# Two-layer diffusion trunk on one core: how many steps of attention and of the time mixing's preparation are written beside each step of layer 0's projections

## The chip, the cores and the metric

One core of a Trainium2 chip runs the whole program. The metric is the device time of one execution in microseconds (us), as the median over runs. Beside the times there is a hardware profile of one execution; all engine times below come from it.

## The reference, cut to what matters

512 latent tokens and 256 context tokens of width 1024 go through two layers. Each layer has a mixer with two groups of heads and an MLP. The change lies in the mixer of layer 0. Its input projection gives both groups their inputs: the group of the time mixing (RWKV-7, a recurrence in both directions with a 64x64 state per head) and the group of the windowed attention (eight query heads over two key/value heads, a band of 128 tokens to either side, the context keys, and a sink logit).

```python
def even_mixer(u_ctx, u_lat, w_in, w_out, a_prm, sink, rope_ang, need_ctx):
    p_ctx = u_ctx @ w_in
    p_lat = u_lat @ w_in
    a_lat, a_ctx = rwkv7_mixer(p_ctx[..., :A_IN], p_lat[..., :A_IN], a_prm, need_ctx)
    ...
    b_lat = banded_window_attention(ql, kl, vl, kc, vc, sink_g)
    out_lat = jnp.concatenate([a_lat, b_lat], axis=-1) @ w_out
...
def rwkv7_scan(f, d, s0, reverse):
    def step(state, inp):
        r_t, w_t, k_t, v_t, kk_t, a_t = inp
        sa = jnp.einsum('bhvk,bhk->bhv', state, -kk_t)
        state = (state * w_t[:, :, None, :] + sa[..., None] * (kk_t * a_t)[:, :, None, :]
                 + v_t[..., None] * k_t[:, :, None, :])
        return state, jnp.einsum('bhvk,bhk->bhv', state, r_t)
```

The kernel doesn't step through the tokens. It cuts them into 12 chunks of 64, solves a triangular system within each chunk, and passes the state from chunk to chunk.

## The kernel before, in words

Everything is fp32; a weight is split into a high and a low part (`split`, lines 182 and 225: ScalarE writes the high part, VectorE the low one), and a product is three matmuls per 128 rows of the contraction. Tokens lie along the free dimension, features on the partitions.

**Generators and steps.** The program is written as Python generators. Each `yield` ends a step, and the code that drives them decides how many steps of one generator are written between two steps of another. Outside the opening, which is scheduled by hand, this order is a rank and not yet the order on an engine: a planner at compile time takes for each engine the instruction of the earliest rank among those whose inputs and buffers are there by its own estimate, so work of a later rank fills holes. On the chip each engine then follows its list in order, and a DMA queue does so too.

**The projections of layer 0.** `columns` (with `product`, line 430) makes 21 column blocks of 128 features; a block is two products, one for the 512 latent and one for the 256 context tokens, of 24 matmuls each. A step is 8 matmuls, so a block is six steps. Blocks 19, 20 and 15 come in the opening and block 16 in six steps of their own (`C0`); from there the counter `n` of the loop around the change starts at 24 and ends at 126. The blocks come in the order 17, 18, 0, 1, ... 14. `done` puts a block through ScalarE and, for blocks 0 to 14, two VectorE operations per product that mix in the neighbouring tokens (lines 1428 and 1429), and a DMA on ScalarE's queue stores it in the scratch tensor `scr`. The weights come through a `Stream`: `load` (line 238) issues 512 KB loads on SP's queue into two raw buffers, `ahead` splits them into three pairs of buffers.

**The attention of layer 0.** `attend` over `units_b`: four pairs of heads, six blocks of 128 queries each, so 24 items. An item has scores (lines 493 and 494), the two mask additions (656, 658), the maximum (499), the exponential (ScalarE), transposes of the probabilities (511), the product with the values (530) and a rescaling (531, 664), in a software pipeline of five steps per item. With eight steps of setting up, two at the start and four at the end it has 128 steps.

**The preparation of the time mixing.** `prep(p, ...)` for the four pairs p of heads. Up to the mark `FRONT` it has 12 steps: loads k and r (lines 849, 850), a norm (405, 415, and a power on GpSimd, 264), two low-rank products (865), two scans (877, 879), exponentials. From there to `READY` it has 18: the factors of the chunks (903 to 908 and 940 to 948; some on GpSimd) and the triangular matrices (917, 918), which go to DRAM and come back in another layout (925, 928; tile N). Then 15 steps hold an inversion of 31 pairs of dependent VectorE operations (954, 955), whose result is copied (958) and goes through DRAM again (959 to 967). Past the mark `MERGE` four steps merge 32x32 blocks into 64x64 ones (974, 982). `first` is the front of pair 0, the rest of pair 0 up to `MERGE`, and the front of pair 1: 57 steps. The buffers of the factors of pair 1 (`st1`) are opened on the side that the projections' inputs and weights have left.

**Behind the projections.** What is left of `first`, then the rest of pair 1 up to `READY`, then the merging of pair 0, with steps of `ada` (line 353 and 362: the modulation vectors of both layers, 80 loads of 512 KB on SP's queue) between them. Then comes for each pair the pass over the chunks (`chunks`, line 1023 first), with the next pairs' preparation beside it, and behind it the output projection and the MLP.

**The loop around the change** (in `trunk`, lines 1446 to 1460) drives the three: per step of the projections `RATE1` steps of attention; when the attention has ended and `n` is over 75, `RATE2` (1.5) turns per step go to `first`, in the order shown in the section on the change.

Of the kernel before, what the change touches and what calls it, by code (L numbers as in the profile page):

```python
# [25 lines left out]
NEG = -1.0e30  # L26
EM05 = math.exp(-0.5)

RATE1, RATE2, RATE3, RATE4, RATE5 = 2.0, 1.5, 1.8, 0.7, 0.5
QUIET = "quiet"  # L30
FRONT = "front"
READY = "ready"
# [142 lines left out]
def trunk(ctx: ExitStack, tc: tile.TileContext, xT, cT, vec_d, wada, we, wo_in, wout, wf1, wf2, lw2_d, la2_d, lg2_d,  # L175
# [5 lines left out]
    def act(o, i, f=AF.Copy, **k):  # L181
        return S.activation(o, i, f, **k)  # L182

    def pool(name, bufs=1, **k):
        return tc.tile_pool(name=name, bufs=bufs, reuse_waits="tile", **k)
# [26 lines left out]
    def one():  # L212
        if PS[0] is None:
            return wide()[:, 0:512]
        return PS[0].tile([128, 512], F32, name="x1")
# [219 lines left out]
    def columns(W, ms, uh, ul, done, parts=lambda m: ((0, L), (L, T))):  # L435

        for m in ms:
            w = W.take()
            for n, (a, b) in enumerate(parts(m)):
                ps = yield from product(w, uh, ul, a, b)  # L440
                if n == 0:
                    W.ahead(1)
                done(m, a, b, ps)
                yield
# [126 lines left out]
    def units(us, n):  # L571

        items = None
        g = us[0]
        while True:
            try:
                next(g)
                yield None
            except StopIteration as e:
                items = e.value  # L580
                break
        for u in range(len(us)):
            g, nxt = (us[u + 1] if u + 1 < len(us) else None), None
            for it in items:
                yield it
                for _ in range(n):
                    if g is not None:
                        try:
                            next(g)
                        except StopIteration as e:  # L590
                            g, nxt = None, e.value
            while g is not None:
                try:
                    next(g)
                    yield None
                except StopIteration as e:
                    g, nxt = None, e.value
            items = nxt
# [230 lines left out]
    def mix_lora(R):  # L829
        for j, a in enumerate((R["wl"], R["al"])):  # L830
            nc.sync.dma_start(a, scr[j])
        act(R["wl"], R["wl"], AF.Tanh)
# [421 lines left out]
    def drain(*gs, fill=lambda: None):  # L1254

        gs = list(gs)
        while gs:
            for g in list(gs):
                if next(g, gs) is gs:
                    gs.remove(g)  # L1260
            fill()
# [21 lines left out]
    def first():  # L1283
        yield from front(0)
        yield from until(preps[0], MERGE)
        yield from front(1)
    early = None
    with psum(2, 2), pool("pat", 2, space=PSUM) as pat, pool("wp", side="right") as wp, pool("ub", 1, side="right") as ub:
# [52 lines left out]
        with tc.manual_schedule(engines=ORDERED):  # L1341
# [27 lines left out]
            def some(ps, w, a, b, k0, k1):  # L1369
                for n, (x, y) in enumerate(three(lambda k: w[0][:, k, :], lambda k: w[1][:, k, :],  # L1370
                                                 lambda k: uh[k][:, a:b], lambda k: ul[k][:, a:b], k1, k0)):
                    PE.matmul(ps[:, 0:b - a], x, y, start=k0 + n == 0, stop=k1 == KT and n == 3 * (k1 - k0) - 1)
# [45 lines left out]
        with pool("po", 1, side="right") as pp:  # L1418
            bt = btx.enter_context(pool("bt", 1, side="right"))
            cur = {}  # L1420

            def done(m, a, b, ps):
                if a == 0:
                    cur[m] = pp.tile([128, T], F32, name="po", bufs=3)
                o = cur[m]
                if m < 15:
                    act(o[:, a:b], ps[:, 0:b - a], scale=om[:, m:m + 1])
                    stt(o[:, a + 1:b], ps[:, 0:b - a - 1], VV["mup"][:, m:m + 1], o[:, a + 1:b], op0=ALU.mult, op1=ALU.add)
                    stt(o[:, a:b - 1], ps[:, 1:b - a], VV["mun"][:, m:m + 1], o[:, a:b - 1], op0=ALU.mult, op1=ALU.add)
                else:  # L1430
                    act(o[:, a:b], ps[:, 0:b - a], scale=0.125 if m < 19 else 1.0)
                if b == T:
                    nc.scalar.dma_start(scr[m], o)
            for n, m in enumerate(ms[:3]):
                done(m, 0, L, first_ps[n])
            for n, m in enumerate(ms[:3]):
                ps = one()
                some(ps, ws[n], L, T, 0, KT)
                W.ahead(min(n + 1, 2))
                done(m, L, T, ps)  # L1440
            cg = columns(W, ms[3:], uh, ul, done)
            for _ in range(C0):
                next(cg)
            mk = lambda: pat.tile([128, 512], F32, name="ax")
            ab = attend(bt, units(units_b(bt), 1), mk, 5)
            n, due = 24, 0.0
            while next(cg, "end") != "end":
                n += 1
                due += RATE1 if ab else RATE2
                while due >= 1:  # L1450
                    due -= 1
                    if ab and next(ab, "end") == "end":
                        ab = None
                        btx.close()
                        rt, iv = (mixs[q].enter_context(pool(("rt", "iv")[q - 2])) for q in (2, 3))
                    if ab is None and n > 6 * 12 + 3:
                        if early is None:
                            mix_lora(R)
                            early = first()
                        next(early, None)  # L1460
            if ab:
                drain(ab)
                btx.close()
                rt, iv = (mixs[q].enter_context(pool(("rt", "iv")[q - 2])) for q in (2, 3))
            if early is None:
                mix_lora(R)
                early = first()
# [422 lines left out]
```

## Time and profile before

| | us |
|---|---|
| median of 3 runs | 2064.45 |
| lowest, highest run | 2062.24, 2076.95 |
| the profiled execution | 2066.39 |
| its span, first to last instruction | 2064.6 |
| TensorE busy in it | 1926.4 (93%) |
| VectorE busy | 1125.7 (55%) |
| ScalarE busy | 818.1 (40%) |

The span is the time from the first to the last instruction; 1.8 us of the execution lie around it. An engine's share is a mean over all stages: here the stages of layer 0's mixer have holes on TensorE, while the MLPs fill it, so the share alone doesn't tell what a change in one stage is worth. PEclk is the clock that TensorE was granted, as a part of 2.4 GHz; 0.5 is 1.2 GHz. PE is TensorE, DVE VectorE, ACT ScalarE, POOL GpSimd; PEld the loading of weights into the array; SPq SP's DMA queue.

### The profile page before, as it was taken

Reading aid. Unit: us, or ns where it says so; the run is one execution under the profiler, and the core shown is the slowest. Engines: PE = TensorE matmul, PEld = TensorE weight load, DVE = VectorE, ACT = ScalarE, POOL = GpSimd, SP = SyncE. Lnnn points to the kernel's source line nnn. Section 1 sums busy time; section 2 is a strip of 40 time slices with the busy share of each in tenths; the row PEclk is TensorE's granted clock in tenths of the full one; section 3 lists DMA queues with packets and bytes.
Section 4 is the critical chain, followed back from the end, with each engine's and each line's share of the span. In section 5 each row is a group of like instructions: output and inputs, shape, how many; then the busy total and the mean of one; then the engine's idle time right before and its main releaser. Section 6 shows DMA issues by size and latency. Waiting matters only on the chain.

```text
span 2064.6 us, 38578 instructions
## 1 busy us (share of the span) xinstructions
PE 1926.4 (93%) x16412; PEld 1630.6 (79%) x16412; DVE 1125.7 (55%) x1999; ACT 818.1 (40%) x1531; POOL 124.3 (6%) x149
## 2 busy tenths in 40 slices
PE   5999986798988899999999999899999899999997
PEld 3888774565667798888888889898888798888887
DVE  6576568556555468234433444865565676444445
ACT  3365533434335345312311232445686645222232
POOL 1000012001100000000000000001121000000000
PEclk9999988798898999999999999999999999999998
DMA  7421234676554223302221121332111425322321
GB/s 308 148 91 62 95 103 130 184 214 194 180 152 125 79 101 123 113 31 82 75 69 42 62 82 42 103 122 91 37 46 37 133 93 174 100 85 82 95 90 41
DMA packets 112012, 217.45 MB, mean 105 GB/s; under 512 B 38496, under 2 KB 63968, under 8 KB 111328
## 3 DMA queue, kind: packets, MB, share of 16 engines
q1 hardware_dynamic: 96544, 191.66, 28.9%
q10 hardware_dynamic: 15296, 23.33, 3.2%
q8 instruction: 128, 2.10, 0.4%
q14 instruction: 44, 0.36, 0.1%
HBM read 184.29 MB, written 28.05 MB: 103 GB/s over the span
## 4 chain that ended last, share of the span: by engine, by line
PE 63%; DVE 7%; ACT 3%; issue 2%; DMA 2%; POOL 1%; ACTq 0%; POOLq 0%; DVEq 0%; SPq 0%
PE x L1587 45%; PE x L430 5%; PE ax L530 2%; PE ax L511 2%; PE ad L353 1%; DMA w_raw<-in_wada_dram 1%; PE b L1015 1%; PE b L493 1%; PE b L494 1%; DVE pr L954 1%; PE b L1077 1%; DVE X L955 1%; DVE nacc L288 1%; ACT Z L182 0%; DVE MQ L1116 0%
## 5 line engine op out<-in xcount | busy, mean ns | idle before, releaser
L182 ACT ACTIVATE w_hi<-w_raw 128x1024 fp32r<-128x1024 f32 x183 | 192.1, 1057 | 476.6 <-PE x L1587 367.1
L225 DVE TENSOR_TENSOR w_lo<-w_raw,w_hi 128x1024 fp32r<-128x1024 f32 x181 | 222.1, 1230 | 196.7 <-ACT w_hi L182 196.1
L1587 PE MATMUL x<-fl,w_hi 128*128 128x256 f32 (+1 forms) x864 | 291.6, 339 | 3.9 <-DVE fl L1674 3.9
L1587 PE MATMUL x<-fh,w_lo 128*128 128x256 f32 (+1 forms) x864 | 289.9, 337 | 0.0
L1587 PE MATMUL x<-uh,w_hi 128*128 128x512 f32 (+1 forms) x864 | 286.9, 337 | 3.0 <-ACT uh L182 3.0
L1587 PE MATMUL x<-ul,w_hi 128*128 128x512 f32 (+1 forms) x864 | 287.4, 336 | 0.0
L1587 PE MATMUL x<-fh,w_hi 128*128 128x256 f32 (+1 forms) x864 | 287.3, 338 | 0.0
L1587 PE MATMUL x<-uh,w_lo 128*128 128x512 f32 (+1 forms) x864 | 287.1, 335 | 0.0
L1601 DVE TENSOR_TENSOR oa<-x,oa 128x512 f32<-128x512 f32 (+1 forms) x184 | 103.1, 563 | 207.7 <-PE x L1587 207.0
L430 PE MATMUL x<-uh,w_hi 128*128 128x256 f32 (+1 forms) x560 | 190.4, 340 | 0.9 <-ACT po L182 0.5
L430 PE MATMUL x<-uh,w_lo 128*128 128x256 f32 (+1 forms) x560 | 188.5, 337 | 0.0
L430 PE MATMUL x<-ul,w_hi 128*128 128x256 f32 (+1 forms) x560 | 188.5, 337 | 0.0
L1587 PEld LDWEIGHTS x<-fl,w_hi 128*128 128x128 f32 x864 | 165.1, 191 | 22.1 <-DVE fl L1674 4.5
L1587 PEld LDWEIGHTS x<-fh,w_lo 128*128 128x128 f32 x864 | 164.8, 191 | 17.8
L1587 PEld LDWEIGHTS x<-uh,w_hi 128*128 128x128 f32 x864 | 161.7, 189 | 21.2 <-ACT uh L182 3.9
L1587 PEld LDWEIGHTS x<-fh,w_hi 128*128 128x128 f32 x864 | 162.5, 190 | 19.9 <-ACT fh L182 2.5
L1587 PEld LDWEIGHTS x<-ul,w_hi 128*128 128x128 f32 x864 | 162.5, 189 | 17.7
L1587 PEld LDWEIGHTS x<-uh,w_lo 128*128 128x128 f32 x864 | 162.4, 189 | 17.6
L430 PEld LDWEIGHTS x<-uh,w_hi 128*128 128x128 f32 x560 | 107.2, 191 | 10.8 <-issue 1.1
L430 PEld LDWEIGHTS x<-uh,w_lo 128*128 128x128 f32 x560 | 107.3, 192 | 9.2 <-issue 1.0
L430 PEld LDWEIGHTS x<-ul,w_hi 128*128 128x128 f32 x560 | 107.2, 191 | 8.5 <-issue 0.5
L1673 DVE TENSOR_TENSOR rl<-rl 128x512 f32<-128x512 f32 (+1 forms) x108 | 59.3, 551 | 73.8 <-ACT fh L182 73.6
(304 smaller groups left out, 3383.7 us busy)
## 6 DMA issues: line engine op xcount, KB each, us to landing
w_raw<-in_wf_dram SPq DMA_DIRECT2D x128, 512.0 KB
w_raw<-in_wada_dram SPq DMA_DIRECT2D x96, 512.0 KB
w_raw<-in_we_dram SPq DMA_DIRECT2D x21, 512.0 KB
w_raw<-in_wo_in_dram SPq DMA_DIRECT2D x18, 512.0 KB
w_raw<-in_wout_dram SPq DMA_DIRECT2D x16, 512.0 KB
hsc<-h ACTq DMA_DIRECT2D x8, 1024.0 KB
scr<-po ACTq DMA_DIRECT2D x21, 384.0 KB
h<-hsc SPq DMA_DIRECT2D x7, 1024.0 KB
```

Of the source, the lines that this page charges most:

```text
L182: return S.activation(o, i, f, **k)
L225: eng.tensor_tensor(o_lo, x, o_hi.bitcast(F32), op=ALU.subtract)
L288: V.tensor_reduce(acc, sq.rearrange("p k t -> p t k"), axis=AX.X, op=ALU.add)
L353: PE.matmul(ps[o:o + 32, 0:256], si[:, 2 * kp + k, :], w[:, k, j * 256:(j + 1) * 256], start=kp == 0, stop=kp == 3)
L430: PE.matmul(ps[:, 0:b - a], x, y, start=j == 0, stop=j == len(pairs) - 1)
L493: PE.matmul(ps[:, off:off + n], qs, kh, start=True, stop=False)
L494: PE.matmul(ps[:, off:off + n], qs, kl, start=False, stop=True)
L511: PE.transpose(pt[:, (kb - k0) * 128:(kb - k0 + 1) * 128], P[:, kb * 128:(kb + 1) * 128], ident)
L530: PE.matmul(po[h * 64:h * 64 + 64, 0:128], v(h, k), pts[h][:, k], start=k == 0, stop=k == n - 1)
L1587: PE.matmul(o, a, b, start=n == 0, stop=n == len(pairs) - 1)
L1601: tt(oa[:, m, tok], ps, oa[:, m, tok], op=ALU.add)
L1673: tt(r, r, r, op=ALU.mult)
```

## The change

Two places: the number of attention steps per step of the projections goes from 2 to 3, and each turn of the preparation is two steps and not one. `RATE1` is used at this place alone.

```diff
-RATE1, RATE2, RATE3, RATE4, RATE5 = 2.0, 1.5, 1.8, 0.7, 0.5
+RATE1, RATE2, RATE3, RATE4, RATE5 = 3.0, 1.5, 1.8, 0.7, 0.5
...
             while next(cg, "end") != "end":
                 n += 1
                 due += RATE1 if ab else RATE2
                 while due >= 1:
                     due -= 1
                     if ab and next(ab, "end") == "end":
                         ab = None
                         btx.close()
                         rt, iv = (mixs[q].enter_context(pool(("rt", "iv")[q - 2])) for q in (2, 3))
                     if ab is None and n > 6 * 12 + 3:
                         if early is None:
                             mix_lora(R)
                             early = first()
-                        next(early, None)
+                        for _ in range(2):
+                            next(early, None)
```

## Rows read from the trace of the kernel before

**Rows 1.** Windows: length, busy us of PE, PEld, DVE, ACT, POOL, clock, DMA share, GB/s

```profile
97.00:253.00 156.00, 155.12 (x1147) 128.36 (x1146) 101.55 (x253) 91.38 (x220) 8.08 (x26) 1.00 0.24 82
254.00:295.00 41.00, 33.14 (x236) 26.28 (x237) 29.64 (x34) 17.29 (x25) 9.51 (x4) 0.83 0.35 119
334.00:376.00 42.00, 18.88 (x371) 12.26 (x370) 24.89 (x51) 8.91 (x18) 9.48 (x6) 0.60 0.69 195
376.00:462.00 86.00, 77.34 (x1386) 53.28 (x1388) 50.28 (x115) 33.95 (x65) 6.58 (x9) 0.96 0.64 196
```

**Rows 2.** Timeline of PE, 253 to 376 us: start, us, what, idle before

```profile
256.60 2.40 PE L405 MATMUL x<-con,t 128*128 128x2 f32 x12 [3.00 <-ACT t L182]
...
290.14 1.14 PE L917 MATMUL b<-ar,bk 64*64 64x64 f32 x32 [5.13 <-DVE XI L918]
...
301.19 0.40 PE L430 MATMUL x<-uh,w_hi 128*128 128x512 f32 x1
...
309.53 0.40 PE L430 MATMUL x<-uh,w_hi 128*128 128x512 f32 x1
...
333.91 0.28 PE L430 MATMUL x<-uh,w_lo 128*128 128x256 f32 x1
...
367.55 2.76 PE L974 MATMUL b<-xw,XI 32*32 32x32 f32 x92 [1.85 <-DMA xw<-tscr]
...
375.92 1.54 PE L1023 MATMUL b<-con,bk 128*128 128x128 f32 x6
```

**Rows 3.** Timeline of DVE, 255 to 385 us

```profile
292.13 0.68 DVE L918 TENSOR_TENSOR XI<-b,con 128x512 f32<-128x512 f32 x1
...
309.04 0.18 DVE L954 TENSOR_TENSOR pr<-X,N 96x31 f32<-96x31 f32 x1
...
357.86 1.03 DVE L958 COPY N<-X 96x1024 f32<-96x1024 f32 x1
374.91 0.19 DVE L954 TENSOR_TENSOR pr<-X,N 96x31 f32<-96x31 f32 x1 [16.02 <-DMA N<-nscr]
```

**Rows 4.** Groups of DVE, 309 to 360 us: busy us, mean ns, idle before

```profile
L955 DVE TENSOR_TENSOR X<-X,pr 96x31 f32<-96x31 f32 (+15 forms) x31 | 12.9, 417 | 0.5
L954 DVE TENSOR_TENSOR pr<-X,N 96x31 f32<-96x31 f32 (+15 forms) x31 | 10.4, 336 | 0.4
...
L1429 DVE SCALAR_TENSOR_TENSOR po<-x,vec,po 128x511 f32<-128x511 f32 (+1 forms) x6 | 3.6, 607 | 0.0
```

**Rows 5.** Groups of PE, ACT and DVE in the attention's stretch, 97 to 253 us

```profile
L430 PE MATMUL x<-uh,w_hi 128*128 128x256 f32 (+1 forms) x145 | 50.3, 347 | 0.0
...
L182 ACT ACTIVATE P<-b,nmx 128x513 f32<-128x513 f32 (+2 forms) x48 | 31.3, 654 | 22.6 <-DVE nmx L499 15.9 <-DVE b L660 4.8 <-DVE sm L554 0.9
...
L225 DVE TENSOR_TENSOR w_lo<-w_raw,w_hi 128x1024 fp32r<-128x1024 f32 x9 | 11.0, 1222 | 2.2 <-ACT w_hi L182 2.0
```

**Rows 6.** Windows of layer 1's attention, columns as in rows 1

```profile
1508.00:1560.00 52.00, 51.21 (x418) 42.23 (x417) 36.91 (x62) 43.07 (x89) 14.63 (x14) 1.00 0.09 27
...
1612.00:1664.00 52.00, 45.49 (x380) 40.60 (x378) 24.38 (x45) 27.72 (x59) 2.17 (x6) 1.00 0.33 104
```

**Rows 7.** Timeline of SP's DMA queue, 200 to 440 us: start, time of the issues

```profile
281.83 0.33 SPq L849 DMA_DIRECT2D k<-scr  x1
282.91 0.33 SPq L238 DMA_DIRECT2D w_raw<-in_we_dram  x1
```

**Rows 8.** Waits of SP's queue, 200 to 420 us: total, times, longest

```profile
SPq L849 <- POOL t L940: 26.4, 2, 23.4
```

**Rows 9.** Timeline of POOL, 60 to 440 us

```profile
247.89 0.95 POOL L930 MEMSET X<- 96x1024 f32 x1
...
336.88 2.02 POOL L940 TENSOR_TENSOR kds<-ic,k 128x768 f32<-128x768 f32 x1 [14.76 <-ACT ic L182]
...
342.87 4.07 POOL L940 TENSOR_TENSOR t<-ic,k 128x768 f32<-128x768 f32 x1 [3.49 <-issue]
348.15 1.82 POOL L947 TENSOR_TENSOR kds<-kds,t 128x768 f32<-128x768 f32 x1 [1.21 <-DVE bk L942]
```

## The prediction, made before the changed kernel was run

> **What bounds the kernel now.** I first read the windows over layer 0's mixer [rows 1]. While the attention runs beside the projections (97 to 253 us) TensorE is busy 155.12 of 156 us at full clock: nothing is to be had there but a different mixture of the same work. Between 334 and 376 us it is busy 18.88 of 42 us, at a mean clock of 0.60. That is the hole the change can reach. The timeline of TensorE [rows 2] gives its edges: the last matmul of the projections starts at 333.91, and the pass over the chunks of pair 0 starts at 375.92. VectorE's timeline [rows 3] says what holds the hole open: the matrices of pair 0 are done at 292.81, their return through DRAM lets the inversion start at 309.04, it ends with the copy at 357.86 to 358.89, its result goes through DRAM again, and only at 367.55 do the merges start on TensorE. So the end of layer 0's mixer hangs on one chain: front of pair 0, matrices, DRAM, inversion, DRAM, merges, chunks. TensorE's other work (the projections) runs out 42 us before this chain is through. Smaller losses stand at the chain's start: 3.00 us before the norm of pair 0 and 5.13 us at the third group of matrices [rows 2], in a stretch with a clock of 0.83 [rows 1].
>
> **The change, part by part.** No instruction is added or removed. What moves is the rank of the attention's and of the preparation's steps, and with it the place of their DMAs on SP's queue.
>
> *Counting.* A step of the projections on TensorE is a sixth of a block: (309.53 - 301.19)/6 = 1.39 us [rows 2], alone and at full clock. The stretch of 97 to 253 us holds 3 x 145 = 435 of its matmuls [rows 5] (the other two groups of line 430 count 145 each too), that is 435/8 = 54.4 steps or 75.6 us. The remaining 156 - 75.6 = 80.4 us are the attention's. Since a block ends at 253 us with n = 90, n was about 36 at 97 us.
>
> *Three attention steps.* Before, 128 steps at two per step end at n = 24 + 64 + 1 = 89; after, at n = 24 + 43 = 67. TensorE's work up to any n stays the same, only sorted differently, so at n = 76 the clock on the wall shows 97 + 80.4 + (76 - 36) x 1.39 = 233.4 us. The same sum to n = 90 gives 252.5, where the trace has 253.
>
> *Two steps of preparation.* The gate `n > 75` never bound before, since the attention ended at 89. Now it does: `first` begins at n = 76. Its norm matmuls, at 256.60 before [rows 2], come at about 234. At 1.5 turns of two steps the 57 steps are all written by n = 95, where they took until n = 126.
>
> *The chain, moved.* From the norm to the last matrix it took 292.81 - 256.60 = 36.2 us. Most of this is waiting from engine to engine, so I leave its length: 234 + 36 = 270. DRAM took 309.04 - 292.81 = 16.2 us: N is there at 286. The inversion was stretched to 48.8 us because VectorE had 51 us of work in that time [rows 4] (the smaller groups of that view left out there): 23.3 for the inversion itself (12.9 + 10.4), 6.5 for the projections' mixing (3.6 of them in line 1429), 5.3 for the front of pair 1, 14.2 for pair 1's factors, and small ones. Now the factors of pair 1 can't be there yet: their buffers need the projections' room. When do the projections end? From 233.4 on TensorE has 50 x 1.39 = 69.5 us of them, about 9 for pair 0's front and matrices, 6 for pair 1's front, and 5 of stall as before: 323 us. At 286 some four blocks are left, which cost VectorE four times (four mixings of 0.61 [rows 4] and one split of 1.22 [rows 5]), 14.6 us. Inversion 20.8 (see the port, below), front of pair 1 5.3, blocks 14.6: 41 us, so the inversion ends at 327 and its copy at 328. From the copy's end to the main merges it took 367.55 - 358.89 = 8.7 us, from there to the chunks 375.92 - 367.55 = 8.4. The chunks start at 345, where they started at 375.9: 30 us earlier.
>
> *What is late next, and what is given back.* Between 323 and 337 TensorE has only pair 1's matrices and the modulation's matmuls, so a hole of some 14 us stays. Pair 1's factors (14.2 us of VectorE) start at 323 and end near 342, before the first VectorE work of the chunks. Its inversion, from 375 on before [rows 3], would run from about 362 inside pair 0's chunks (345 to 431) as it did before. The modulation's matmuls that filled the old hole must go elsewhere: at most their 9 us at the low clock, at least nothing, since pair 0's chunks leave 8.7 of 86 us idle [rows 1]; I take 3.
>
> *A denser attention.* Where TensorE finds the attention not ready it waits, because its list is fixed. Before it lost 0.9 us in the stretch. After, the same 80.4 us of attention lie beside 31 steps instead of 54, in about 123 us. ScalarE was busy 91 of 156 us [rows 1]; if all 91 were the attention's, that is 74% of 123. Lower bound nothing. Upper bound: where layer 1's attention runs short of projections TensorE idles 6.5 of 52 us [rows 6], which for 123 us is 15. The nearer row is the one in which ScalarE is busy 83% and TensorE still 51.21 of 52: 1.5%, so I take 2 us.
>
> *SP's queue.* The load of pair 1's k (281.83) waited 23.4 us for GpSimd to release pair 0's [rows 8], and a weight load stood right behind it [rows 7]. After the change more weight loads stand behind such waits: three blocks' more. The cover is two raw and three split buffers, some 25 us or more of projections at 8.3 us per block. I cost it at nothing; without the cover the price is a wait of up to 23 us.
>
> *The port of VectorE and GpSimd.* The inversion's 31 updates (line 955) took 417 ns in the mean, its 31 products of the same sizes (954) 336 ns [rows 4]: 2.5 us more in all, while GpSimd worked 2.02 + 4.07 + 1.82 = 7.9 us on pair 1's factors [rows 9]. I read the difference as the cost of that neighbour. After the change these three operations come behind the inversion, hence 23.3 - 2.5 = 20.8. The Trainium skill (SBUF — State Buffer, Who interferes with whom) goes further: it says that a VectorE operation with two SBUF inputs and a GpSimd one that reads SBUF exclude each other for a whole instruction. By that rule up to the whole 7.9 us would be freed, and the forecast would be 5 us lower; the rows show only 2.5 of it.
>
> **Sum.** 30 - 3 - 2 = 25 us. From the profiled execution, 2066.4 - 25 = **2041 us**; the median of the runs is 2 us below that execution, which I leave in the range. Behind layer 0's mixer the page has TensorE busy nine tenths in nearly every slice, so a shift there arrives at the end.
>
> **The rivals.**
>
> *Half of it.* The inversion stays as slow as it was (48.8 us from 286, since its operations alternate with whatever else is ready), and N comes up to 6 us later because more weight loads share the DMA queue. The copy ends at 341, the chunks start at 358: 18 us, less 5 given back: 13, 2053 us. For it: VectorE was without a hole there. Against it: 14 us of that work can't start yet.
>
> *Nothing moves.* The planner fills holes beyond the written order: pair 0's X was cleared at 247.89 [rows 9], before the attention's end. If it had already pulled everything as early as it can go, the rank changes nothing: 2064 us. Against it: TensorE was full until 253, so there rank decided.
>
> *Slower: the attention starves TensorE.* In the stretch from 97 to 220 us the chain scores, maximum, exponential, transposes of an item doesn't keep up with three steps. If TensorE idles there as in the poor window [rows 6] it costs 15 us, and if its clock falls to the 0.83 of the stretch with such holes [rows 1], 0.17 x 123 = 21 more. Against a gain of 27 without the attention's term this ends at 2066 + 36 - 27 = 2075 us. It decides against the change from 27 us on, 1.1 us for each of 24 items. Against it: less than 1 us of waits at two steps.
>
> *More.* The inversion runs almost undiluted and the 5.13 us stall and the low clock around 260 us vanish: 36 us, 2030 us.
>
> **How the numbers follow.** Forecast 0.43, half 0.25, nothing 0.13, slower 0.08, more 0.11. One per cent is 20.6 us, about what a measurement of this kernel can tell from none: the forecast passes it four times in five (0.35), "more" always, "half" one time in five (0.05): faster 0.51. The starving attention passes it on the other side less than half the time, and I add a little for an order that falls badly: 0.05. The rest, 0.44, is within it. The range leaves out the far part of "more" and the slower half of the starving: 2026 to 2066.
>
> **What would show it.** Right: attention's last item near 220 to 225, line 405 near 234, the inversion's first operation near 286, the chunks' first transposes near 345, the projections ending near 323, and from there on all stages shifted by the same amount. Wrong: waits of TensorE on ScalarE or VectorE between 97 and 225 (starving), line 405 still near 256 (nothing moves), an inversion that ends past 335 (half), or a pass over pair 0's chunks that takes more than the 86 us it took (given back).

## The result, and the profile after

The kernel after takes 2056.1 us (median of 14 runs, 2047.9 to 2069.0), the kernel before 2066.8 beside it (14 runs, 2057.0 to 2078.5): a ratio of 0.995, interval 0.993 to 0.9969, some 10 us faster. The forecast was 2041. The direction was right, the 25 us were more than twice the gain. The profiled execution took 2055.19 us with a span of 2053.4.

Windows of after, columns as in [rows 1]:

```profile
97.00:226.00 129.00, 128.68 (x975) 103.24 (x974) 86.76 (x234) 81.45 (x209) 9.34 (x26) 1.00 0.23 74
...
243.00:253.00 10.00, 9.53 (x23) 5.00 (x24) 5.20 (x6) 2.50 (x3) 0.00 (x0) 0.50 0.25 92
...
288.00:304.00 16.00, 16.00 (x42) 9.94 (x41) 12.43 (x26) 9.24 (x12) 0.00 (x0) 0.50 0.00 0
304.00:346.00 42.00, 42.00 (x248) 36.78 (x246) 28.26 (x64) 9.69 (x15) 2.96 (x3) 1.00 0.37 107
346.00:365.00 19.00, 13.05 (x339) 9.12 (x338) 14.28 (x21) 6.39 (x15) 4.69 (x3) 0.75 0.73 213
365.00:449.00 84.00, 74.22 (x1372) 53.50 (x1370) 51.64 (x118) 34.56 (x65) 6.68 (x9) 0.96 0.63 197
```

The denser attention ends at 226 us almost without a hole (128.68 of 129). The hole of 42 us in [rows 1] has become one of 19, and the pass over pair 0's chunks is no longer than before. But two stretches stand among the projections in which TensorE is full and its clock is 0.50, that is 1.2 GHz: 9.53 + 16.00 us of work there would take half as long at full clock, 12.8 us less. The timeline of TensorE says what stands in front of each:

```profile
238.80 1.47 PE L405 MATMUL x<-con,t 128*128 128x2 f32 x12
...
243.47 1.54 PE L415 MATMUL b<-con,t 128*128 128x128 f32 x6 [1.98 <-DVE t L412]
244.94 2.93 PE L865 MATMUL b<-wl,lw 64*128 64x512 f32 x4
...
287.47 1.51 PE L415 MATMUL b<-con,t 128*128 128x128 f32 x6 [2.36 <-DVE pr L954]
288.91 4.10 PE L865 MATMUL b<-wl,lw 64*128 64x512 f32 x8
...
303.54 0.63 PE L430 MATMUL x<-uh,w_lo 128*128 128x512 f32 x1
...
304.33 0.40 PE L430 MATMUL x<-ul,w_hi 128*128 128x512 f32 x1
...
345.78 0.28 PE L430 MATMUL x<-uh,w_lo 128*128 128x256 f32 x1
...
348.81 0.69 PE L917 MATMUL b<-ar,bk 64*64 64x64 f32 x8 [2.40 <-DVE po L1429]
352.08 1.12 PE L917 MATMUL b<-ar,bk 64*64 64x64 f32 x28 [2.59 <-DVE bk L908]
...
357.05 1.99 PE L974 MATMUL b<-xw,XI 32*32 32x32 f32 x96
...
364.70 1.54 PE L1023 MATMUL b<-con,bk 128*128 128x128 f32 x6
```

Behind each norm (line 405) the transposes (415) wait 1.98 and 2.36 us, and the clock is down to half from there on; after the second wait a matmul of 512 columns takes 0.63 us until 303.54 and 0.40 from 304.33. The projections end at 346, later than the 334 of [rows 2]. The main merges start 10.5 us and the chunks 11.2 us earlier than in [rows 2]. VectorE's timeline:

```profile
268.60 0.68 DVE L918 TENSOR_TENSOR XI<-b,con 128x512 f32<-128x512 f32 x1
...
287.24 0.18 DVE L954 TENSOR_TENSOR pr<-X,N 96x31 f32<-96x31 f32 x1
...
329.90 1.13 DVE L958 COPY N<-X 96x1024 f32<-96x1024 f32 x1
...
381.44 0.18 DVE L954 TENSOR_TENSOR pr<-X,N 96x31 f32<-96x31 f32 x1
```

Against [rows 3] the matrices are 23 us earlier, the inversion starts 22 and its copy 28 us earlier. So pair 0's chain came as far ahead as forecast, and lost 17 us of it between the copy and the chunks: the merges wait behind pair 1's matrices (line 917) in TensorE's list, and these wait for the end of the projections.

### The profile page after: what moved, and what is told of

Read it like the earlier page. It is cut to its first block, busy times and chain, and to the rows that moved or that the text cites. A ratio compares the mean times of both kernels' runs of the same rounds, so it can differ in the third digit from the quotient of the medians.

```text
span 2053.4 us, 38620 instructions
## 1 busy us (share of the span) xinstructions
PE 1932.7 (94%) x16412; PEld 1633.5 (80%) x16412; DVE 1124.7 (55%) x1999; ACT 817.0 (40%) x1531; POOL 122.2 (6%) x149
## 4 chain that ended last, share of the span: by engine, by line
PE 63%; DVE 7%; ACT 3%; issue 3%; DMA 2%; POOL 1%; POOLq 0%; ACTq 0%; DVEq 0%; SPq 0%
PE x L1588 45%; PE x L430 5%; PE ax L530 2%; PE ax L511 2%; PE b L1015 1%; PE b L493 1%; PE ad L353 1%; PE b L1077 1%; PE b L494 1%; DMA w_raw<-in_wada_dram 1%; DVE X L955 1%; DVE nacc L288 1%; ACT Z L182 1%; DVE pr L954 1%; POOL r L264 0%
```

## The experiments

The table has what the timelines of TensorE show: the end of the projections, the first transposes of pair 0's first and second batch of chunks, and the first merges of pairs 1 and 3 (us). A ratio is to the runs of before that were taken beside the kernel's own. The marks come from the one profiled execution, which can lie up to 10 us from the median (att2_prep2_vkr 2074.2 against 2063.8, after_late_ada 2065.1 against 2071.8): marks of two kernels that lie few us apart tell nothing.

| kernel | median (runs) | ratio, interval | proj. end | batch 1 | batch 2 | merges 1 | merges 3 |
|---|---|---|---|---|---|---|---|
| before | 2066.8 (14) | | 334 | 375.9 | 390.5 | 462.6 | 637.2 |
| after | 2056.1 (14) | 0.995, 0.993 to 0.9969 | 346 | 364.7 | 375.8 | 448.3 | 622.3 |
| att3_prep1 | 2077.8 (12) | 1.0047, 1.0031 to 1.0064 | 348 | 366.9 | 410.7 | 479.1 | 650.7 |
| att2_prep2 | 2065.6 (12) | 0.9996, 0.9979 to 1.0012 | 342 | 363.4 | 397.4 | 468.1 | 640.9 |
| room16 | 2059.7 (12) | 0.9955, 0.9934 to 0.9975 | 331 | 347.8 | 387.8 | 454.9 | 626.1 |
| merge_first | 2054.2 (8) | 0.9935, 0.9912 to 0.9958 | 348 | 365.6 | 375.6 | 445.2 | 625.3 |
| room16_late_ada | 2059.4 (12) | 0.9971, 0.9952 to 0.999 | 332 | 348.5 | 365.0 | 440.6 | 629.7 |
| after_late_ada | 2071.8 (10) | 1.0021, 1.0004 to 1.0038 | 348 | 363.5 | 374.9 | 440.6 | 635.2 |
| before_late_ada | 2080.9 (4) | 1.0071, 1.0055 to 1.0088 | 335 | 374.7 | 386.7 | 455.6 | 652.1 |
| room16_v | 2056.5 (4) | 0.9945, 0.9923 to 0.9967 | 329 | 345.7 | 379.8 | 454.4 | 625.2 |
| room16_spread | 2066.5 (12) | 0.9991, 0.9969 to 1.0012 | 330 | 347.0 | 363.5 | 435.6 | 634.0 |
| after_spread | 2080.4 (7) | 1.0054, 1.003 to 1.0077 | 347 | 363.2 | 374.3 | 444.3 | 647.7 |
| room16_merge_spread | 2058.9 (12) | 0.996, 0.9942 to 0.9979 | 328 | 344.2 | 355.0 | 424.0 | 622.3 |
| **room16_vkr** | **2043.1 (6)** | 0.9861, 0.9833 to 0.9889 | 330 | 348.0 | 360.8 | 434.1 | 607.0 |
| after_vkr | 2053.4 (7) | 0.9934, 0.9908 to 0.9959 | 347 | 366.5 | 376.4 | 448.8 | 620.1 |
| before_vkr | 2072.5 (12) | 1.0015, 0.9998 to 1.0033 | 335 | 377.0 | 391.5 | 465.2 | 634.9 |
| room_merge_vkr | 2045.2 (6) | 0.9881, 0.9857 to 0.9906 | 334 | 353.9 | 364.7 | 433.9 | 607.4 |
| att3_prep1_vkr | 2055.2 (5) | 0.993, 0.9907 to 0.9954 | 341 | 361.5 | 375.0 | 449.9 | 626.7 |
| att2_prep2_vkr | 2063.8 (10) | 0.9979, 0.9961 to 0.9997 | 340 | 367.0 | 378.8 | 465.0 | 638.0 |

**The halves of the change, alone.**

```diff
-RATE1, ... = 2.0, ...                          # att3_prep1, from before
+RATE1, ... = 3.0, ...
-RATE1, ... = 3.0, ...                          # att2_prep2, from after
+RATE1, ... = 2.0, ...
```

> The attention's half of the change alone: three attention steps, one step of preparation per turn. Theory A (the change's gain comes from the attention making room, and the second step per turn only costs TensorE waits and clock between 239 and 304 us): line 405 stays near 239, the waits before line 415 are no longer than 2 us in all, the projections end between 333 and 342 (346 with both halves), the chunks start between 352 and 362, time 2045 to 2054. Rival B (the second step per turn is what brings the chain forward): N and the inversion come 8 us or more later than with both halves (N at 295 or later), the chunks start at 365 or later, time 2056 to 2063.

> The preparation's half alone: two attention steps, two steps of preparation per turn. Theory A: line 405 at 256 as before, since the attention still ends at n = 89; the projections end at or after 334 (before: 334) because of added waits before line 415; the chunks start between 368 and 380, time 2058 to 2070, no better than 0.5% under the kernel before. Rival B: most of the gain is here, chunks at 366 or earlier, time 2052 to 2058.

Neither half gains, and one loses, though both start the chunks 9 and 12 us earlier than before. In both the second batch comes 44 and 34 us behind the first, against 15 in before. Why had to stay open here; the last two runs answer it for att3_prep1 and in part for att2_prep2. Att3_prep1 is slower than both its theory and its rival; att2_prep2 has the time of its theory, with chunks that start as early as its rival had them. The waits in front of line 415 are there in both: 1.98 and 1.73 us in att3_prep1, 1.72 and 1.35 in att2_prep2. So it isn't the second step of the preparation alone that brings them.

**Room between the norm and its transposes.** In the list of after only six and seven projection matmuls stand between lines 405 and 415 (in before eight, at the low clock, and eleven, without a wait over 0.9 us), and in that time GpSimd's power (2.27 us) and two short VectorE operations have to come. Room16 writes 16 empty steps there.

```diff
         pow_mhalf(r12[:, :2 * nt], n12[:, :2 * nt], 2 * nt)
-        yield
+        for _ in range(1 + room):              # room=16 for pairs 0 and 1, else 0
+            yield
```

> Both halves, and 16 empty steps in the preparation of pairs 0 and 1 between the norm's matmuls (line 405) and the transposes that wait for GpSimd's power (line 415 in the changed kernel). They put some 35 matmuls of the projections behind the norm where 6 and 7 stood. Theory A (TensorE's end of the projections moved from 334 to 346 us because of the waits for the power and the low clock that follows each): both waits before the transposes gone (4.4 us), TensorE at full clock from 282 to 304 in place of 0.5, the projections end between 332 and 339, the chunks start between 348 and 358, time 2042 to 2051. Rival C (the waits are short and the low clock has another cause, such as the small matmuls of the low-rank products): the waits go but the clock stays low there, the projections end at 341 or later, time 2053 to 2058. Rival D (the chain of the time mixing is the bound, not TensorE): the empty steps delay the chain by 5 us, the chunks start at 368 or later, time 2058 to 2063.

The first half of the matter is settled by windows of room16 that answer to those of after:

```profile
239.00:270.00 31.00, 28.47 (x244) 22.96 (x243) 21.40 (x29) 14.28 (x22) 6.57 (x4) 1.00 0.25 85
270.00:310.00 40.00, 38.13 (x209) 30.51 (x208) 34.17 (x63) 18.60 (x24) 3.68 (x2) 1.00 0.42 129
...
348.00:455.00 107.00, 89.99 (x1454) 60.80 (x1456) 53.78 (x122) 35.83 (x68) 7.25 (x10) 0.82 0.69 211
```

The waits in front of the transposes are gone, the clock is 1.00 throughout beside the same low-rank matmuls (rival C falls), and the projections end at 331 instead of 346: 15 us, against 4.3 of waits and 12.8 of low clock in after. The chunks start at 347.8, 28 us before [rows 2]. Yet nothing of this arrives: the pass over pair 0 takes 107 us instead of the 86 of [rows 1].

**Merges first.**

```diff
-        for t in until(preps[1], READY):
-            next(ag, None)
         for t in preps[0]:
             next(ag, None)
+        for t in until(preps[1], READY):
+            next(ag, None)
```

> Both halves, and the merges of pair 0 written before pair 1's matrices behind the projections instead of after them. Theory A (from 346 on the chunks wait because the merges, whose data is there by 339, stand behind pair 1's matrices in TensorE's list): the merges start between 346 and 349 (357 with the change), the chunks between 352 and 358 (364.7), time 2046 to 2052. Rival E (pair 1's matrices have to be done anyway, and the time moves into the pass over the chunks): the chunks start early but the merges of pair 1 (448 with the change) don't come earlier by over 3 us, time 2054 to 2059.

The merges start at 350.9 instead of 357.1, the chunks at 365.6 as in after, and its time can't be told from that of after, as rival E had it: with projections that end at 348, the order behind them makes no difference that shows.

**Where room16 loses it: the modulation.** Timeline of TensorE in room16, between the two batches:

```profile
357.26 0.73 PE L353 MATMUL ad<-w_raw,si 128*32 128x256 f32 x8 [2.37 <-DMA w_raw<-in_wada_dram]
359.39 1.08 PE L353 MATMUL ad<-w_raw,si 128*32 128x256 f32 x8 [1.41 <-DMA w_raw<-in_wada_dram]
...
373.57 2.03 PE L353 MATMUL ad<-w_raw,si 128*32 128x256 f32 x16 [0.33 <-DVE mod L364]
375.96 0.89 PE L1041 MATMUL b<-con,vr 128*128 128x128 f32 x3 [0.37 <-POOL vr L1039]
...
387.82 1.54 PE L1024 MATMUL b<-con,bk 128*128 128x128 f32 x6
```

and of SP's queue in room16:

```profile
355.51 14.31 SPq L341 DMA_DIRECT2D w_raw<-in_wada_dram  x8
369.87 0.43 SPq L1001 DMA_DIRECT2D v<-scr  x1
370.35 0.42 SPq L850 DMA_DIRECT2D k<-scr  x1
```

For 18 us TensorE has only the modulation (`ada`, line 353), and a load at a time to wait for. The load of v that pair 0's chunks need stands behind eight modulation loads on the queue. In after it went at 344.65, in before at 332.78. Three kernels write the modulation's steps elsewhere, a fourth moves the load of v.

```diff
         for t in until(preps[1], READY):       # late_ada, spread
-            next(ag, None)
+            pass
         for t in preps[0]:
-            next(ag, None)
+            pass
...
-                due[1] += RATE4                # RATE4 = 0.7
+                due[1] += RATE4                # late_ada: RATE4 = 0.95
+                due[1] += 1.3 if p == 0 else RATE4   # spread: RATE4 = 0.7
```

```diff
-        nc.sync.dma_start(v, scr[3 + 3 * p + 2])              # room16_v, in chunks
+        (nc.sync if p else nc.scalar).dma_start(v, scr[3 + 3 * p + 2])
```

> Room16 with one more edit: none of the modulation's steps is written beside the preparation that stands between the projections and the chunks; the rate beside the chunks goes from 0.7 to 0.95 so that all are still written before the end. Theory (in room16 a bunch of 40 modulation matmuls, each four of them waiting for a 512 KB load, stands in TensorE's list between the first and the second batch of pair 0's chunks, and eight such loads stand on SP's queue ahead of the load of v): the projections end near 331 and the chunks start near 347 as in room16, the second batch's first transposes follow within 14 us instead of 39, the merges of pair 1 start near 436 instead of 454.9, and the time is 2066.9 - 27 = 2040 us, or up to 14 us more where the 22 steps that were pushed back cost TensorE time in a full stretch. Rival (the inversion of pair 1 on VectorE, from 361 to 391 in room16, holds the second batch): the second batch stays later than 380 and the merges of pair 1 later than 448, about 2057 us.

> The kernel after with the same edit (the modulation's steps not written beside the preparation before the chunks, rate 0.95 beside them). The projections end near 346 as before the edit, since nothing in front of them changes. The list of after had no bunch, only twelve matmul groups of the modulation spread among pair 1's matrices and the merges: theory expects the chunks to start 2 to 4 us earlier (361 to 363), the merges of pair 1 at about 445 and 2053 us. If the late end of the projections alone decided everything in after, this is the same as after, 2056; if the modulation's steps were what kept the gain small there too, the merges of pair 1 come before 440 and the time is 2046 or less.

> The kernel before with the same edit on the modulation's steps, as a control. There the chain of pair 0 (inversion until 358, chunks at 376) sets the start of the chunks, not the modulation. Theory: chunks at 372 to 376, merges of pair 1 at 458 to 463, 2062 to 2067 us, no more than 4 us better than before. Rival (moving the modulation is a gain by itself, whatever the change does): 2055 us or less.

> Room16 with the load of v for pair 0's chunks on ScalarE's queue instead of SP's, where eight modulation loads stood ahead of it. Theory (it is the modulation's bunch on TensorE's list that holds the second batch, the load of v is only its companion): the transposes of v come before 355 now, but the second batch still starts near 385 and the merges of pair 1 near 452, about 2058 us. Rival (the load of v alone is what was late): the second batch within 14 us of the first, the merges of pair 1 near 437, about 2042 us.

Room16_late_ada has its second batch at 365 and pair 1's merges at 440.6, 14 us before room16, close to the 436 expected: the inversion of pair 1, the rival, didn't hold the batch. But all of it is lost until pair 3's merges (629.7). The same edit costs before and after some 15 us each, which no theory had: with more of the modulation written beside the later pairs, their passes get longer. The queue has a part in it: the load of pair 2's v went at 571.25 (after_late_ada) and 588.73 (before_late_ada), 21 and 24 us behind the first merges of that pair, where after and before without the edit had it at 511.61 and 523.46, ahead of them. How large that part is wasn't separated. Room16_v shows that v was not the only one: its v went early, and ten loads' worth of the modulation (40 matmuls in the program, 80 records in the trace) then stood in front of the norm of pair 2, whose k and r were still behind eight modulation loads (issued at 369.33 and 369.81). Its second batch comes at 379.8, as expected of the bunch.

**Spreading it evenly.**

> Room16 with none of the modulation's steps beside the preparation in front of the chunks, and the same 22 steps written evenly beside pair 0's chunks instead (rate 1.3 there, 0.7 beside the other pairs as before). Theory (the bunch in room16 cost by its place in front of the second batch, and in room16_late_ada the steps that left pair 0's pass cost the later passes 14 us): projections end near 331, chunks start near 347, second batch near 360, merges of pair 1 near 442 (room16_late_ada 440.6, room16 454.9) and the later passes again 100 and 75 us long, as in room16, instead of 106 and 83: merges of pair 3 near 617 and a time of about 2047 us. Rival (the modulation costs TensorE the same time wherever it stands in these passes, so that nothing is to be had by its order): merges of pair 1 at 450 to 456, merges of pair 3 at 625 to 630, 2056 to 2060 us.

> The kernel after with the same edit (22 steps of the modulation evenly beside pair 0's chunks instead of in front of them). The projections still end near 346 with their two waits and the low clock. Theory: chunks at 363 (after_late_ada 363.5), merges of pair 1 between 445 and 449, later passes 101 and 76 us, 2054 to 2056 us, the same as after: the modulation's place isn't what keeps its gain at 10 us. Rival (it is): merges of pair 1 at 441 and 2048 us or less.

> Room16_spread with the merges of pair 0 written ahead of pair 1's factors and matrices, which stood in front of them in TensorE's list from 334.6 to 340.5 in room16_late_ada while the merges' data was there. Theory: merges at 334 to 336, chunks at 341, the second batch at 356, and, since pair 1's matrices then start after the merges (340) and its N, inversion and factors follow, the merges of pair 1 at 438 to 442: 2043 to 2047 us, 2 to 4 us below room16_spread. Rival (what gates the pass is pair 1's own chain, which moves 4 us later): merges of pair 1 4 us later than in room16_spread, and no gain over it.

The first pass came out better than expected (merges of pair 1 at 435.6, with the merges moved ahead at 424.0), and the pass of pair 1 took 130 us instead of 100. Forecast 2047, measured 2066: a miss. So is room16_merge_spread (2058.9 for 2043 to 2047), whose pass of pair 1 took 123 us. SP's queue in room16_spread shows the same picture one pass later:

```profile
425.45 35.65 SPq L341 DMA_DIRECT2D w_raw<-in_wada_dram  x18
...
475.28 0.38 SPq L1001 DMA_DIRECT2D v<-scr  x1
```

Pair 1's merges had started at 435.6, and the v that its chunks need went at 475. After_spread misses by most, 2080.4 instead of 2054 to 2056. There pair 2's matrices were ready at 445, and their stores stood behind 21 loads of the modulation; the pass of pair 1 took 125 us:

```profile
421.98 53.50 SPq L341 DMA_DIRECT2D w_raw<-in_wada_dram  x21
475.53 4.23 SPq L925 DMA_DIRECT2D nscr<-XI  x4
```

This points away from how much of the modulation stands where, and to DMAs on which the chain depends and which queue behind it.

**Off the queue.** The loads of v (all pairs), and of k and r (pairs 2 and 3) go to ScalarE's queue. No step is moved.

```diff
-        nc.sync.dma_start(v, scr[3 + 3 * p + 2])        # in chunks
+        nc.scalar.dma_start(v, scr[3 + 3 * p + 2])
...
-        nc.sync.dma_start(k, scr[3 + 3 * p + 1])        # in prep
-        nc.sync.dma_start(r, scr[3 + 3 * p])
+        q = nc.sync if p < 2 else nc.scalar
+        q.dma_start(k, scr[3 + 3 * p + 1])
+        q.dma_start(r, scr[3 + 3 * p])
```

> Room16 with the loads of v for every pair's chunks and of k and r for pairs 2 and 3 on ScalarE's queue instead of SP's, where the modulation's loads stand. No step is moved. Theory (these loads stood behind eight modulation loads of earlier rank, and the list of TensorE filled the wait for them with 40 modulation matmuls): the projections end near 331, chunks start near 347, the second batch near 360 instead of 388, the pass over pair 0 lasts 87 us plus up to 8 for its 60 more modulation matmuls, so the merges of pair 1 start at 436 to 443 instead of 454.9, the later passes last 100 and 75 us as in room16, and the time is about 2047 us. Rival (the stretch is bound by TensorE's total work, an order can't help): merges of pair 1 at 448 or later, or later passes that give it back, and 2055 us or more.

> The kernel after with the same edit on the queues of v, k and r. Its list had no bunch: v went at 344.65 and k of pair 2 at 350.23, both ahead of the modulation's loads; only r of pair 2 stood behind seven of them and was not missed. Theory: no difference, merges of pair 1 within 3 us of 448, 2054 to 2058 us. Rival (the queue cost after something as well): 2050 us or less.

> The kernel before with the same edit, as a control: v went at 332.78 and k of pair 2 at 346.96, ahead of the modulation's loads, so nothing changes: 2064 to 2069 us, merges of pair 1 within 3 us of 462.6. Rival (the edit is a gain by itself): 2060 us or less.

> A kernel meant to be the fastest: 8 empty steps behind the norm's power instead of 16, the merges of pair 0 written ahead of pair 1's factors and matrices, and v, k and r off SP's queue. Theory: the projections end between 331 and 340, the merges follow the return of the inversion's result without pair 1's matrices in front of them, so that the chunks start at 341 to 348, no bunch follows, merges of pair 1 at 436 to 444 and 2043 to 2050 us. Rival (the merges moved ahead only delay pair 1's chain by as much): merges of pair 1 no earlier than in room16_vkr and no gain over it.

ScalarE's timeline of room16_vkr has v's load at 330.19, k's at 334.31 and r's at 342.91. TensorE's has no bunch any more:

```profile
348.03 1.54 PE L1025 MATMUL b<-con,bk 128*128 128x128 f32 x6
...
359.00 1.50 PE L405 MATMUL b<-con,t 128*128 128x2 f32 x12
360.76 0.87 PE L1025 MATMUL b<-con,bk 128*128 128x128 f32 x6 [0.26 <-DVE n L856]
```

and its window of the pass, which answers to the third of room16's:

```profile
348.00:434.00 86.00, 77.53 (x1382) 55.12 (x1378) 48.26 (x116) 32.97 (x64) 7.13 (x9) 0.94 0.66 195
```

The pass is back at 86 us. Room16_vkr takes 2043.1 us, 0.9861 of before, 4 us better than expected and 10 us better than after_vkr beside it, with the intervals apart. The same edit does nothing for after that its interval tells, and nothing good for before, whose loads went in time. The place of these loads on the queue is shown as the cause: one edit, and of these three only the kernel whose loads were late gains. Whether it acts more on the chip or through the list that the planner makes by its own estimate of these loads isn't separated. Room_merge_vkr (8 empty steps, merges first) is no faster; its rival was right.

> Three attention steps and one step of the preparation, with v, k and r off SP's queue. Theory (the queue's order was the loss): chunks near 367 as in att3_prep1, but the pass over pair 0 86 to 92 us instead of 112, merges of pair 1 at 453 to 459 instead of 479, 2055 to 2063 us instead of 2077.8. Rival (this half loses by itself): merges of pair 1 at 465 or later, 2066 us or more.

> Two attention steps and two steps of the preparation, with v, k and r off SP's queue. Theory: chunks near 363 as in att2_prep2, the pass over pair 0 86 to 92 us instead of 105, merges of pair 1 at 449 to 455 instead of 468, 2052 to 2058 us instead of 2065.6. Rival: merges of pair 1 at 462 or later, 2064 us or more.

In the traces without the edit v, k and r went at 392 us in att3_prep1, k and r at 388 in att2_prep2, each time behind eight modulation loads. Three attention steps alone go from 2077.8 to 2055.2 us, with a pass of 88 us instead of 112. That is as fast as after_vkr (2053.4): the second step of the preparation adds nothing that can be told. Not all of it is the queue: the projections end at 341 instead of 348, mostly because the low clock behind the second wait was shorter (last section). Of the other half only a part came back: its second batch follows 12 us behind the first again, but its pass takes 98 us instead of the 86 to 92 expected, and 2063.8 us is above its range; merges of pair 1 at 465.0 are what its rival had. In that pass TensorE waits 7.5 us for the modulation's own loads (2.3 in room16_vkr's), at a mean clock of 0.89 (0.94). Why they come late there stays open.

## Why the prediction was right or wrong

- **Counting and attention: right.** Line 405 came at 238.80 (234 forecast; the sum that says 233.4 gives 233.0). The dense attention cost 0.3 us of waits and not 2; the starving rival falls.
- **The chain: right.** Matrices 269 (270), inversion from 287 (286), copy from 329.9 (328).
- **The port: right as read from the row.** With GpSimd idle beside it, the 31 updates of line 955 took a mean of 335 ns against the 417 of [rows 4], 2.5 us in all. The group in after (287 to 331 us), and the two updates of before that make up the difference:

```profile
L955 DVE TENSOR_TENSOR X<-X,pr 96x31 f32<-96x31 f32 (+15 forms) x31 | 10.4, 335 | 0.7
...
345.30 1.84 DVE L955 TENSOR_TENSOR X<-X,pr 96x175 f32<-96x175 f32 x1
...
348.76 1.38 DVE L955 TENSOR_TENSOR X<-X,pr 96x156 f32<-96x156 f32 x1
```

  Each ended 0.2 us behind a GpSimd operation of [rows 9] (346.94 and 349.97), where updates of their sizes take 0.31 and 0.32 us in after. That agrees with the rule of the Trainium skill (SBUF — State Buffer, Who interferes with whom) that the two exclude each other; but only two of the 31 updates were held, so that 2.5 us came back and not its upper bound of 7.9.
- **"323 us" for the end of the projections: this step failed,** by 23 us. The sum had "5 of stall as before" and full clock. I had seen a clock of 0.83 in the same stretch of before [rows 1] and put the price of a wait at its length. Two waits, 4.3 us together, cost 12.8 more in clock; room16 gives 15 back. Of the other 8, 5 are the later line 405; 3 stay unexplained. The kernel before could have shown the gap: the same sum from its n = 90 at 253 us (36 x 1.39 + 9 + 6 + 5) gives 323 as well, where its projections ended at 334. The step also left out that the stalls could get worse: between a norm and its transposes the list of after has six and seven projection matmuls, that of before eight and eleven. Att3_prep1 has six and four, so this comes with the attention's half as well.
- **"8.7 us from the copy to the merges": failed with it.** It was 26 (331.0 to 357.05), since pair 1's matrices stand in front of the merges and wait for the projections.
- **3 us given back: right for after,** whose pass takes 84 us. It was the wrong bound all the same, and luck that it held: it priced the modulation's matmuls, and the section on SP's queue priced weight loads alone. The modulation's 80 loads stand on that queue too, and with the chunks 28 us earlier (room16) the pass took 21 us longer behind them.
- **The rivals.** "Half of it" has nearly the measured time (2053) by a mechanism that didn't happen: the inversion wasn't slow. The 25 us are there: with both obstacles away (room16_vkr) the chunks start 28 and pair 1's merges 28.5 us earlier, and 24.7 us arrive in the time.

## What to carry to other kernels

When a chain is written earlier, look at each place where another engine answers TensorE within it and count what is left to do in TensorE's list meanwhile: the waits of 1.98 and 2.36 us there cost 2.4 and 3.4 times their length again in clock, though others cost less (last section). And ask, for each load of the chain, what stands in front of it on its queue once the chain comes earlier: bulk loads that only fill holes belong on another queue than the loads that the chain waits for. A gain that an experiment brings at the start of a stage should be followed to the stage's end before it is counted.

## What the runs showed that was not expected

After a wait of 2.36 us TensorE worked 16.00 of 16 us without a hole at 0.50 of its clock before it was granted the full one again, and 9.53 of 10 after one of 1.98. But the loss doesn't follow the length of the wait. In after the waits of 1.44 and 1.28 us at 263 and 267 us left the clock at 1.00. In before the low stretch was shorter behind the wait of 5.13 us (second line) than behind that of 3.00 (first line):

```profile
256.60:266.50 9.90, 9.90 (x35) 7.32 (x35) 1.74 (x3) 0.98 (x2) 2.27 (x1) 0.66 0.65 231
290.14:294.40 4.26, 4.26 (x40) 3.46 (x41) 3.06 (x5) 0.00 (x0) 0.00 (x0) 0.50 0.24 66
```

And behind the same wait of 1.73 us, in front of the same matmuls, att3_prep1 (first line) stayed at 0.50 for three times as long as att3_prep1_vkr, which is back at full clock from 313 us:

```profile
309.10:324.90 15.80, 15.76 (x34) 9.63 (x35) 10.50 (x18) 5.25 (x6) 0.00 (x0) 0.50 0.06 25
306.70:311.70 5.00, 4.93 (x13) 3.50 (x14) 4.93 (x12) 0.00 (x0) 0.00 (x0) 0.50 0.20 79
```

So the price of such a wait can't be told in advance from its length; that it can be more than its length is what the forecast lacked.
